# A two-layer decoder trunk: the FFN's block products written out as a software pipeline on VectorE, ScalarE and TensorE

## The chip, the cores and the metric

The kernel runs on one core of a Trainium2 chip. The metric is device time in microseconds (us) of one execution, median of several; lower is better.

## The reference

The computation is a trunk of two layers, each a gated token mixer and then a dense SwiGLU feed-forward network (FFN), on 512 tokens of width 1024, in float32. The change touches the FFN alone:

```python
D_MODEL = 1024; SEQ = 512; DEPTH = 2
FF = ((8 * D_MODEL + 3 * 256 - 1) // (3 * 256)) * 256        # 2816

def _swiglu(h, w_gate_up, w_down):
    gu = jnp.einsum('bsd,df->bsf', h, w_gate_up)
    g, u = gu[..., :FF], gu[..., FF:]
    return jnp.einsum('bsf,fd->bsd', jax.nn.silu(g) * u, w_down)

def reference(x, norm_mix, w_in, w_ret_o, w_sb_o, w_out, norm_ffn, w_gate_up, w_down, norm_final):
    h = x
    for layer in range(DEPTH):
        hn = _rmsnorm(h, norm_mix[layer])
        h = h + _mixer(hn, w_in[layer], w_ret_o[layer], w_sb_o[layer], w_out[layer])
        hn = _rmsnorm(h, norm_ffn[layer])
        h = h + _swiglu(hn, w_gate_up[layer], w_down[layer])
    return _rmsnorm(h, norm_final)
```

## The kernel before

**Numbers.** Every float32 operand of a product is split into a high and a low part. ScalarE (ACT) writes the high part as a rounded copy, VectorE (DVE) subtracts it from the original for the low part, and TensorE (PE) multiplies high x high, low x high and high x low into one PSUM sum. So a weight tile is ready for PE when it has been loaded into a raw buffer (SP issues the load; three buffers, `rawp`), copied by ACT (`whi`, or `w_h` for half a tile) and subtracted by DVE (`wlo`, `w_l`). The wide pairs `whi`, `wlo` have three buffers each.

**The FFN.** The 2816 features are 22 tiles of 128. For each, a gate product and an up product of 512 tokens are made, silu(gate) x up is formed, split (`a_h`, `a_l`), and the down projection sums over features. The first five tiles (PLAIN) are plain: two units of 24 matmuls of 512 columns each. While they run, `pair_input` prepares sums of the normed input for the other seventeen. These, called pairs here (tiles 5 to 21 of a layer), use a product scheme with seven block products in place of eight. A block (`block`, whose matmuls carry L613) is twelve matmuls of 256 columns; a pair is 84. The blocks are named by their weights: A11 and A12 (halves of the gate tile a), A22 (a half of the up tile b), S1 to S4 (sums of halves). Gate and up results, g and u, lie in two PSUM banks: `x` (named g in the trace) takes A11, S2, S3, A22, and `zy` (named a) takes A12, S1, S4. On the way ACT copies two partial sums out of `x`: into `pu` after A11 (L624) and after S2 (L628), each before the next block may add to the same sum; and into `u3` after S3 (L632), which DVE adds to S1's sum (L633). At the end DVE adds `zy` and `pu` (L638), ACT takes silu (L639), DVE multiplies to `a` (L646) and ACT copies `a_h` (L647).

**A pair's weights** (`pair_weights`, L555 to L579) come from two loads, a and b, of 512 KB: `whi`, `wlo` of a (L565, L566; for A11, A12); `s1`, a sum of b's halves (L571); A22's split (L237, L238); two subtractions in place (L573, L574); `whi`, `wlo` of the changed b (S3, S2); S1's split; one more sum (L577); and S4's split. The load of a later tile waits until a raw buffer's last reader is done.

**What sets the order.** A scheduler orders each engine's instructions; the source order is a preference, and the functions are generators that interleave a pair's blocks with the last two of the pair ahead. An engine runs its own list one after the other. `down(0)` (features 0 to 10) comes after pair 12, and `down(1)` after pair 21; each is eight tiles of 33 matmuls of 512 columns, and the first tile of each has its own loop (L700 to L720), since its newest `a_h` comes last.

## Time and profile before

| | |
|---|---|
| median of 3 runs | 1651.94 us (1651.32 to 1652.76) |
| the profiled execution | 1651.83 us, of which its span is 1650.1 us |
| PE busy | 1626.0 us, 99 % of the span |
| DVE, ACT busy | 1134.4 us (69 %), 799.9 us (48 %) |
| granted PE clock, mean | 0.999 of full speed |

The profile is of one execution. PE's busy time uses modelled ends: a matmul of 256 columns is shown as 0.28 us and the next one starts 0.12 us after it, so a small gap doesn't show as idle time. The start times of the timeline do show it. The pairs of the first layer run from 516 to 602 and from 663 to 762 us, those of the second from 1331 to 1417 and from 1478 to 1577 us.

### The profile page before, as it was taken

What the parts mean: (1) busy time and instruction counts of PE and PEld (TensorE: products, weight loads), DVE (VectorE), ACT (ScalarE), POOL (GpSimd) and SP (SyncE); (2) the same over time, 40 slices, a digit from 0 to 9 for tenths busy, and PEclk for the clock granted to TensorE, in tenths of its full rate; (3) what the DMA queues carried; (4) which work ended last, traced back from release to release, by engine and by line L of the source; (5) the groups of instructions that cost most, each with busy time, mean ns of one, the idle gap of its engine ahead of it and who ended that gap; (6) DMA issues with size and microseconds to landing.
All of it is one profiled execution on the core that took longest, in us unless ns stands there. A gap on an engine that the chain in (4) does not pass through costs nothing.

```text
span 1650.1 us, 21859 instructions
## 1 busy us (share of the span) xinstructions
PE 1626.0 (99%) x8665; PEld 1376.0 (83%) x8665; DVE 1134.4 (69%) x1657; ACT 799.9 (48%) x1307; POOL 67.9 (4%) x57
## 2 busy tenths in 40 slices
PE   9999999999999999999999999999999999999998
PEld 7887777888888988998888778888888889889977
DVE  5799878645577774776448987885354877648753
ACT  5667745432354542454327677453234545325543
POOL 2000000000210000000200000000002000000001
PEclk9999999999999999999999999999999999999999
DMA  5322311233222333233332122123222313332332
GB/s 195 103 77 77 101 54 64 90 102 103 92 77 89 97 111 100 86 95 108 111 100 90 64 90 90 63 68 103 99 96 96 103 64 93 111 104 80 97 106 77
DMA packets 47911, 153.62 MB, mean 93 GB/s; under 512 B 5440, under 2 KB 5952, under 8 KB 47808
## 3 DMA queue, kind: packets, MB, share of 16 engines
q1 hardware_dynamic: 45360, 148.00, 27.7%
q10 hardware_dynamic: 2448, 4.22, 0.8%
q8 instruction: 68, 1.11, 0.3%
q14 instruction: 35, 0.29, 0.1%
HBM read 150.10 MB, written 2.10 MB: 92 GB/s over the span
## 4 chain that ended last, share of the span: by engine, by line
PE 86%; DVE 10%; ACT 2%; issue 1%; DMA 0%; ACTq 0%; SPq 0%; DVEq 0%
PE g L84 18%; PE g L83 18%; PE g L85 18%; PE g L613 12%; PE a L613 8%; PE g L115 2%; PE g L116 2%; PE g L117 2%; DVE wlo L69 2%; DVE z L371 1%; PE a L85 1%; DVE rt L299 1%; PE a L84 1%; PE a L83 1%; DVE kl L345 1%
## 5 line engine op out<-in xcount | busy, mean ns | idle before, releaser
L67 ACT ACTIVATE whi<-raw 128x1024 fp32r<-128x1024 f32 (+1 forms) x224 | 220.2, 983 | 445.8 <-PE g L84 270.0
L69 DVE TENSOR_TENSOR wlo<-raw,whi 128x1024 fp32r<-128x1024 f32 (+1 forms) x224 | 255.1, 1141 | 112.4 <-ACT whi L67 111.7
L84 PE MATMUL g<-xl,whi 128*128 128x512 f32 x800 | 312.4, 391 | 0.0
L85 PE MATMUL g<-xh,wlo 128*128 128x512 f32 x800 | 311.8, 390 | 0.0
L83 PE MATMUL g<-xh,whi 128*128 128x512 f32 x800 | 309.9, 391 | 0.7 <-ACT xh L173 0.7
L83 PEld LDWEIGHTS g<-xh,whi 128*128 128x128 f32 x800 | 150.1, 188 | 33.0 <-ACT xh L173 1.6
L85 PEld LDWEIGHTS g<-xh,wlo 128*128 128x128 f32 x800 | 150.2, 188 | 31.0
L84 PEld LDWEIGHTS g<-xl,whi 128*128 128x128 f32 x800 | 150.2, 188 | 30.8
L85 PE MATMUL g<-a_h,wlo 128*128 128x512 f32 (+1 forms) x319 | 122.3, 383 | 1.5 <-DVE wlo L69 1.5
L84 PE MATMUL g<-a_l,whi 128*128 128x512 f32 (+1 forms) x319 | 123.4, 387 | 0.0
L83 PE MATMUL g<-a_h,whi 128*128 128x512 f32 (+1 forms) x319 | 122.7, 385 | 0.0
L232 POOL TENSOR_TENSOR acc<-acc,sq 128x512 f32<-128x512 f32 x34 | 54.1, 1590 | 1074.4 <-ACT sq L231 1073.9
L565 ACT ACTIVATE whi<-raw 128x1024 fp32r<-128x1024 f32 x68 | 69.0, 1055 | 52.0 <-DVE raw L574 46.0
L613 PE MATMUL a<-xf_h,w_l 128*128 128x256 f32 x272 | 79.6, 293 | 3.2 <-DVE w_l L238 2.9
L566 DVE TENSOR_TENSOR wlo<-raw,whi 128x1024 fp32r<-128x1024 f32 x68 | 80.8, 1222 | 1.1 <-ACT whi L565 1.1
L613 PE MATMUL g<-xf_h,whi 128*128 128x256 f32 x272 | 79.8, 293 | 0.3
L613 PE MATMUL g<-xf_h,wlo 128*128 128x256 f32 x272 | 76.3, 281 | 0.0
L613 PE MATMUL g<-xf_l,whi 128*128 128x256 f32 x272 | 76.2, 280 | 0.0
L115 PE MATMUL g<-whi,xh 128*128 128x512 f32 x192 | 74.9, 392 | 1.0 <-ACT v L318 1.0
L117 PE MATMUL g<-wlo,xh 128*128 128x512 f32 x192 | 75.0, 390 | 0.0
L116 PE MATMUL g<-whi,xl 128*128 128x512 f32 x192 | 74.9, 390 | 0.0
L613 PE MATMUL a<-xf_l,w_h 128*128 128x256 f32 x272 | 71.7, 281 | 0.0
(230 smaller groups left out, 3623.5 us busy)
## 6 DMA issues: line engine op xcount, KB each, us to landing
raw<-in_wgu SPq DMA_DIRECT2D x88, 512.0 KB, 3.3
raw<-in_wf SPq DMA_DIRECT2D x76, 512.0 KB, 3.3
raw<-in_wt SPq DMA_DIRECT2D x24, 512.0 KB, 3.3
raw<-in_wdn SPq DMA_DIRECT2D x32, 384.0 KB, 3.2
raw<-in_wdn SPq DMA_DIRECT2D x32, 320.0 KB, 2.9
raw<-in_wro SPq DMA_DIRECT2D x16, 512.0 KB, 3.2
raw<-in_wout SPq DMA_DIRECT2D x16, 512.0 KB, 3.3
raw<-in_wsb SPq DMA_DIRECT2D x8, 512.0 KB, 3.3
```

The costliest lines, as they stand in the source:

```text
L67: self.last_hi = nc.scalar.activation(hi[:, :n], raw[:, :n], AF.Copy).ins
L69: nc.vector.tensor_tensor(out=lo[:, :n], in0=raw[:, :n], in1=hi[:, :n], op=ALU.subtract)
L83: mm(out, lhsT=ah, rhs=bh, start=start, stop=False)
L84: mm(out, lhsT=ah, rhs=bl, start=False, stop=False)
L85: self.last_mm = mm(out, lhsT=al, rhs=bh, start=False, stop=stop).ins
L115: mm(out, lhsT=ah, rhs=bh, start=start, stop=False)
L116: mm(out, lhsT=al, rhs=bh, start=False, stop=False)
L117: mm(out, lhsT=ah, rhs=bl, start=False, stop=stop)
L232: nc.gpsimd.tensor_tensor(out=self.acc, in0=self.acc, in1=sq, op=ALU.add)
L565: nc.scalar.activation(hi, src, AF.Copy)
L566: tt(out=lo, in0=src, in1=hi, op=ALU.subtract)
L613: self.nc.tensor.matmul(out, lhsT=l[:, s], rhs=r, start=start and c == 0 and k == 0, stop=c == 3 and k == 2, skip_group_check=True)
```

## The change

The block products are the same, and so are the matmuls, copies and sums. What is new is their order and who decides it. `act` and `add` issue ACT and DVE work that the scheduler must keep in the source's order, and the first matmul of each block is kept in order too. A call of `step` does pair f on PE: A11, A12, A22 of the pair ahead, S2, S1, S4 of the pair ahead, S3. Between the blocks the generator `pair_weights` makes the weights of pair f+1, in three parts. `turn`, at the head of a step, finishes earlier pairs: `u3` of f-1, the sum with it, and `a`, `a_h` of f-2. For the first pair the weights are made in the last plain tile (PLAIN-1); for pair 12 in `down(0)`'s last tile. `down(0)` now comes after pair 11, whose last two blocks stay open until step 12, and the first tile of `down(1)` takes its own loads (`down_units`) and several `a_l` from the step before. A few slots changed side in SBUF. The diff, cut to its core:

```diff
+    def add(self, out, a, b, op=ALU.add):
+        return self.tc.keep_in_program_order(self.nc.vector.tensor_tensor(out=out, in0=a, in1=b, op=op))
+    def act(self, out, a, f=AF.Copy):
+        return self.tc.keep_in_program_order(self.nc.scalar.activation(out, a, f))
+    def sub(self, out, a, b):
+        return self.add(out, a, b, ALU.subtract)
...
     def pair_weights(self, gate, up):
-        nc, tt = self.nc, self.nc.vector.tensor_tensor
         a, b = self.raw_unit(gate), self.raw_unit(up)
         p, q = slice(0, T), slice(T, 2 * T)
+        wide = lambda: (self.wp.tile([P, 1024], F32R, name="whi", tag="whi"), self.wp.tile([P, 1024], F32R, name="wlo", tag="wlo"))
+        one = lambda n: (self.slot(n + "h", F32R), self.slot(n + "l", F32R))
+        w = {}
+        ah, al = wide()
+        self.act(ah, a)
+        yield w
         s1 = self.slot("s1")
-        def wide(src):
-            hi, lo = self.wp.tile([P, 1024], F32R, name="whi", tag="whi"), self.wp.tile([P, 1024], F32R, name="wlo", tag="wlo")
-            nc.scalar.activation(hi, src, AF.Copy)
-            tt(out=lo, in0=src, in1=hi, op=ALU.subtract)
-            return [(hi[:, s], lo[:, s]) for s in (p, q)]
-        w = {}
-        w["A11"], w["A12"] = wide(a)
-        tt(out=s1, in0=b[:, p], in1=b[:, q], op=ALU.add)
-        w["A22"] = self.split(b[:, q], "w")
-        tt(out=b[:, p], in0=a[:, p], in1=b[:, p], op=ALU.subtract)
-        tt(out=b[:, q], in0=a[:, p], in1=s1, op=ALU.subtract)
-        w["S3"], w["S2"] = wide(b)
-        w["S1"] = self.split(s1, "w")
-        tt(out=a[:, q], in0=a[:, q], in1=b[:, q], op=ALU.add)
-        w["S4"] = self.split(a[:, q], "w")
-        return w
+        self.add(s1, b[:, p], b[:, q])
+        self.sub(al, a, ah)
+        w["A11"], w["A12"] = ((ah[:, s], al[:, s]) for s in (p, q))
+        h, l = w["A22"] = one("a22")
+        self.act(h, b[:, q])
+        h1, l1 = w["S1"] = one("s1")
+        self.act(h1, s1)
+        self.sub(l, b[:, q], h)
+        self.sub(b[:, p], a[:, p], b[:, p])
+        self.sub(b[:, q], a[:, p], s1)
+        bh, bl = wide()
+        self.act(bh, b)
+        self.add(a[:, q], a[:, q], b[:, q])
+        self.sub(l1, s1, h1)
+        self.sub(bl, b, bh)
+        w["S3"], w["S2"] = ((bh[:, s], bl[:, s]) for s in (p, q))
+        yield
+        h, l = w["S4"] = one("s4")
+        self.act(h, a[:, q])
+        self.sub(l, a[:, q], h)
+        yield
...
-                self.nc.tensor.matmul(out, lhsT=l[:, s], rhs=r, start=start and c == 0 and k == 0, stop=c == 3 and k == 2, skip_group_check=True)
-    def pair(self, wgu, f):
-        nc, tt = self.nc, self.nc.vector.tensor_tensor
-        h = T // 2
-        p, q = slice(0, h), slice(h, T)
-        w = self.pair_weights(wgu[2 * f], wgu[2 * f + 1])
-        x, zy = self.bank(), self.abank()
-        t, u3 = self.slot("pu"), self.slot("u3")
-        self.block(x[:, p], w["A11"], "B11", True)
-        nc.scalar.activation(t[:, p], x[:, p], AF.Copy)
-        self.block(zy[:, p], w["A12"], "B21", True)
-        yield
-        self.block(x[:, p], w["S2"], "T2", False)
-        nc.scalar.activation(t[:, q], x[:, p], AF.Copy)
-        self.block(zy[:, q], w["S1"], "T1", True)
-        yield
-        self.block(x[:, p], w["S3"], "T3", False)
-        nc.scalar.activation(u3[:, p], x[:, p], AF.Copy)
-        tt(out=x[:, q], in0=zy[:, q], in1=u3[:, p], op=ALU.add)
-        yield
-        self.block(x[:, p], w["A22"], "T4", False)
-        yield
-        self.block(zy[:, q], w["S4"], "B22", False)
-        tt(out=t, in0=zy, in1=t, op=ALU.add)
-        nc.scalar.activation(t, t, AF.Silu)
-        self.activated(x, t)
-        yield
-    def activated(self, u, g):
-        a, hi = self.slot("a", F32, self.alow()), self.slot("a_h", F32R, self.alow())
-        self.nc.vector.tensor_tensor(out=a, in0=u, in1=g, op=ALU.mult)
-        self.nc.scalar.activation(hi, a, AF.Copy)
+                mm = self.nc.tensor.matmul(out, lhsT=l[:, s], rhs=r, start=start and c == 0 and k == 0, stop=c == 3 and k == 2, skip_group_check=True)
+                if c == 0 and k == 0:
+                    self.tc.keep_in_program_order(mm)
...
+    def turn(self, prep=None):
+        if self.old:
+            x, zy, t, w = self.old
+            u3 = self.slot("u3")
+            self.act(u3[:, : T // 2], x[:, : T // 2])
+        first = next(prep) if prep else None
+        if self.done:
+            self.activated(*self.done, keep=self.tc.keep_in_program_order)
+        if self.old:
+            self.add(x[:, T // 2 :], zy[:, T // 2 :], u3[:, : T // 2])
+        self.open, self.old, self.done = self.old or self.open, None, None
+        return first
+    def last_products(self):
+        x, zy, t, w = self.open
+        self.block(x[:, : T // 2], w["A22"], "T4", False)
+        yield
+        self.block(zy[:, T // 2 :], w["S4"], "B22", False)
+        self.add(t, zy, t)
+        self.act(t, t, AF.Silu)
+        self.done, self.open = (x, t), None
+        yield
+    def step(self, w, prep, other=lambda: None):
+        p, q = slice(0, T // 2), slice(T // 2, T)
+        nxt = self.turn(prep)
+        behind = self.last_products() if self.open else iter(())
+        x, zy, t = self.bank(), self.abank(), self.slot("pu")
+        self.block(x[:, p], w["A11"], "B11", True)
+        self.act(t[:, p], x[:, p])
+        self.block(zy[:, p], w["A12"], "B21", True)
+        if prep:
+            next(prep)
+        else:
+            other()
+        next(behind, None)
+        self.block(x[:, p], w["S2"], "T2", False)
+        self.act(t[:, q], x[:, p])
+        self.block(zy[:, q], w["S1"], "T1", True)
+        if prep:
+            next(prep)
+        next(behind, None)
+        self.block(x[:, p], w["S3"], "T3", False)
+        self.old = x, zy, t, w
+        return nxt
...
+            if f == PLAIN - 1:
+                prep = weights(PLAIN)
+                w = next(prep)
...
+            if f == PLAIN - 1:
+                next(prep), next(prep)
...
-        old = None
-        for f in range(PLAIN, NF):
-            new = self.pair(wgu, f)
-            next(new)
-            if old:
-                next(old)
-            next(new)
-            if old:
-                next(old)
-            next(new)
-            old = new
-            if f == HALF + 1:
-                self.down(wdn, 0, range(KC))
+        for half in range(2):
+            def lows():
+                self.units = self.down_units(wdn, half, 0)
+                for k in range(EARLY):
+                    self.low_part(half * HALF + k)
+            end = (HALF, NF - 1)[half]
+            for f in range(PLAIN if half == 0 else HALF + 1, end):
+                w = self.step(w, weights(f + 1))
+            self.step(w, None, lows)
+            self.turn()
+            if half == 0:
+                w = self.down(wdn, 0, range(KC), lambda: weights(HALF + 1))
         if last:
             self.tc.keep_in_program_order(nc.scalar.preload_act_table_set("sqrt_and_others"))
-        self.down(wdn, 1, range(KC - 1 if last else KC), old, last)
-    def down(self, wdn, half, tiles, old=None, last=False):
+        self.down(wdn, 1, range(KC - 1 if last else KC), None, last)
...
+                behind = self.last_products() if half else iter(())
+                mm, where = nc.tensor.matmul, {f: (u, slice((f - a) * P, (f - a + 1) * P)) for a, b, u in units for f in range(a, b)}
+                def high(f):
+                    u, s = where[f]
+                    for k in range(2):
+                        mm(ps, lhsT=u[k][:, s], rhs=self.ax[f][0], start=f == f0 and k == 0, stop=False)
+                def low(f):
+                    u, s = where[f]
+                    mm(ps, lhsT=u[0][:, s], rhs=self.ax[f][1], start=False, stop=f == f1 - 1)
+                for f in range(f0 + EARLY, f1 - 1):
+                    self.low_part(f)
+                for f in range(f0, f1 - 1):
+                    if f in (f0 + 4, f0 + 6):
+                        next(behind, None)
+                    high(f)
+                if half:
+                    self.activated(*self.done, keep=self.tc.keep_in_program_order)
+                    self.done = None
+                for f in range(f0, f1 - 1):
+                    low(f)
+                self.low_part(f1 - 1)
+                high(f1 - 1)
+                low(f1 - 1)
             else:
+                if weights and i == tiles[-1]:
+                    prep = weights()
+                    w = next(prep)
+                    next(prep), next(prep)
...
```

Three places show what moves. In the rows the names carry tile numbers, `waits` names the queues or engines whose signals an instruction waits for (DMAHW: a load), and a row without `waits` needs none of its own.

DVE, where the first layer's pairs begin, before: from the last plain gate tile (`g_4372`) on. `u_4406` and `a_4408` are tile 4's, `raw_4412` and `raw_4414` are pair 5's a and b, and `wlo_4515` is pair 6's.

```order
L668 TENSOR_TENSOR g_4372<-g_4347,rs_y_3976 128x512 [waits PE_49]
L672 TENSOR_TENSOR u_4406<-g_4381,rs_y_3976 128x512 [waits PE_49]
L571 TENSOR_TENSOR s1_4416<-raw_4414 128x512 [waits DMAHW1_49]
L646 TENSOR_TENSOR a_4408<-u_4406,g_4372 128x512 [waits DVE_49,Activation_49]
L238 TENSOR_TENSOR w_l_4423<-raw_4414,w_h_4422 128x512 [waits Activation_49]
L573 TENSOR_TENSOR raw_4414<-raw_4412,raw_4414 128x512 [waits DVE_49]
L574 TENSOR_TENSOR raw_4414<-raw_4412,s1_4416 128x512 [waits DVE_49]
L238 TENSOR_TENSOR w_l_4433<-s1_4416,w_h_4432 128x512 [waits Activation_49]
L577 TENSOR_TENSOR raw_4412<-raw_4412,raw_4414 128x512 [waits DVE_49]
L566 TENSOR_TENSOR wlo_4429<-raw_4414,whi_4428 128x1024 [waits Activation_49]
L566 TENSOR_TENSOR wlo_4515<-raw_4509,whi_4514 128x1024 [waits DMAHW2_49,Activation_49]
L238 TENSOR_TENSOR w_l_4438<-raw_4412,w_h_4437 128x512 [waits Activation_49]
```

The same place after; `u_4435` and `a_4437` are tile 4's, `raw_4372` and `raw_4374` pair 5's a and b.

```order
L712 TENSOR_TENSOR g_4379<-g_4347,rs_y_3976 128x512 [waits PE_49]
L553 TENSOR_TENSOR s1_4413<-raw_4374 128x512 [waits DMAHW0_49]
L553 TENSOR_TENSOR wlo_4377<-raw_4372,whi_4376 128x1024 [waits DMAHW7_49]
L553 TENSOR_TENSOR a22l_4417<-raw_4374,a22h_4416 128x512 [waits Activation_49]
L553 TENSOR_TENSOR raw_4374<-raw_4372,raw_4374 128x512 [waits DVE_49]
L553 TENSOR_TENSOR raw_4374<-raw_4372,s1_4413 128x512 [waits DVE_49]
L553 TENSOR_TENSOR raw_4372<-raw_4372,raw_4374 128x512 [waits DVE_49]
L553 TENSOR_TENSOR s1l_4420<-s1_4413,s1h_4419 128x512 [waits Activation_49]
L553 TENSOR_TENSOR wlo_4426<-raw_4374,whi_4425 128x1024 [waits Activation_49]
L553 TENSOR_TENSOR s4l_4432<-raw_4372,s4h_4431 128x512 [waits Activation_49]
L718 TENSOR_TENSOR u_4435<-g_4388,rs_y_3976 128x512 [waits PE_49]
L640 TENSOR_TENSOR a_4437<-u_4435,g_4379 128x512 [waits DVE_49]
```

Tile 4's u and a stood ahead of pair 5's weights; now all of pair 5's weights stand ahead of them.

ACT at the same place, before:

```order
L669 ACTIVATE g_4372<-g_4372 128x512 [waits DVE_49]
L237 ACTIVATE w_h_4422<-raw_4414 128x512 [waits DMAHW1_49]
L237 ACTIVATE w_h_4432<-s1_4416 128x512 [waits DVE_49,Activation_49]
L647 ACTIVATE a_h_4409<-a_4408 128x512 [waits DVE_49,PE_49]
L565 ACTIVATE whi_4428<-raw_4414 128x1024 [waits DVE_49,Activation_49]
L565 ACTIVATE whi_4514<-raw_4509 128x1024 [waits DMAHW2_49,PE_49,Activation_49]
L237 ACTIVATE w_h_4437<-raw_4412 128x512 [waits DVE_49]
L624 ACTIVATE pu_4443<-g_4441 128x256 [waits PE_49]
L628 ACTIVATE pu_4443<-g_4441 128x256 [waits PE_49]
L632 ACTIVATE u3_4444<-g_4441 128x256 [waits PE_49]
```

and after; `a_h_4438` is tile 4's, `whi_4445` pair 6's A11 and A12, and the two `pu_4450` are pair 5's copies after A11 and after S2:

```order
L713 ACTIVATE g_4379<-g_4379 128x512 [waits DVE_49]
L556 ACTIVATE s1h_4419<-s1_4413 128x512 [waits DVE_49,Activation_49]
L556 ACTIVATE whi_4425<-raw_4374 128x1024 [waits DVE_49,PE_49,Activation_49]
L556 ACTIVATE s4h_4431<-raw_4372 128x512 [waits DVE_49]
L641 ACTIVATE a_h_4438<-a_4437 128x512 [waits DVE_49,Activation_49]
L556 ACTIVATE whi_4445<-raw_4441 128x1024 [waits DMAHW2_49,PE_49,Activation_49]
L556 ACTIVATE pu_4450<-g_4448 128x256 [waits PE_49]
L556 ACTIVATE a22h_4479<-raw_4443 128x512 [waits DMAHW3_49]
L556 ACTIVATE s1h_4482<-s1_4476 128x512 [waits DVE_49,Activation_49]
L556 ACTIVATE whi_4488<-raw_4443 128x1024 [waits DVE_49,PE_49]
L556 ACTIVATE pu_4450<-g_4448 128x256 [waits PE_49]
```

Pair 5's copies had ahead of them pair 6's first `whi` and S4's `w_h`; now the first has tile 4's `a_h` and pair 6's `whi` ahead of it, and the second also pair 6's A22, S1 and second `whi`.

DVE, a whole step in the middle of the pairs, before (`raw_4509` and `raw_4511` are pair 6's a and b, `wlo_4642` is pair 7's):

```order
L633 TENSOR_TENSOR g_4441<-a_4442,u3_4444 128x256 [waits Activation_49]
L238 TENSOR_TENSOR w_l_4520<-raw_4511,w_h_4519 128x512 [waits Activation_49]
L573 TENSOR_TENSOR raw_4511<-raw_4509,raw_4511 128x512 [waits DVE_49]
L574 TENSOR_TENSOR raw_4511<-raw_4509,s1_4513 128x512 [waits DVE_49]
L238 TENSOR_TENSOR w_l_4530<-s1_4513,w_h_4529 128x512 [waits Activation_49]
L577 TENSOR_TENSOR raw_4509<-raw_4509,raw_4511 128x512 [waits DVE_49]
L566 TENSOR_TENSOR wlo_4526<-raw_4511,whi_4525 128x1024 [waits Activation_49]
L566 TENSOR_TENSOR wlo_4642<-raw_4636,whi_4641 128x1024 [waits DMAHW4_49,PE_49,Activation_49]
L238 TENSOR_TENSOR w_l_4535<-raw_4509,w_h_4534 128x512 [waits Activation_49]
L638 TENSOR_TENSOR pu_4443<-a_4442,pu_4443 128x512 [waits PE_49]
L646 TENSOR_TENSOR a_4618<-g_4441,pu_4443 128x512 [waits Activation_49]
L571 TENSOR_TENSOR s1_4640<-raw_4638 128x512 [waits DMAHW5_49]
```

and after (`raw_4660` and `raw_4662` are pair 8's, `pu_4547` is pair 6's and `g_4545` pair 6's x; pair 7 is on PE):

```order
L553 TENSOR_TENSOR g_4545<-a_4546,u3_4658 128x256 [waits Activation_49]
L553 TENSOR_TENSOR s1_4700<-raw_4662 128x512 [waits DMAHW7_49,DVE_49]
L553 TENSOR_TENSOR wlo_4665<-raw_4660,whi_4664 128x1024 [waits DMAHW6_49,PE_49,Activation_49]
L553 TENSOR_TENSOR a22l_4704<-raw_4662,a22h_4703 128x512 [waits DVE_49,Activation_49]
L553 TENSOR_TENSOR raw_4662<-raw_4660,raw_4662 128x512 [waits DVE_49]
L553 TENSOR_TENSOR raw_4662<-raw_4660,s1_4700 128x512 [waits DVE_49]
L553 TENSOR_TENSOR raw_4660<-raw_4660,raw_4662 128x512 [waits DVE_49]
L553 TENSOR_TENSOR s1l_4707<-s1_4700,s1h_4706 128x512 [waits Activation_49]
L553 TENSOR_TENSOR wlo_4713<-raw_4662,whi_4712 128x1024 [waits Activation_49]
L553 TENSOR_TENSOR s4l_4756<-raw_4660,s4h_4755 128x512 [waits PE_49,Activation_49]
L553 TENSOR_TENSOR pu_4547<-a_4546,pu_4547 128x512 [waits PE_49]
L640 TENSOR_TENSOR a_4794<-g_4545,pu_4547 128x512 [waits Activation_49]
```

Before, a pair's S1, S3 and S2 weights were made while the pair itself was on PE, and only its A11 `wlo` one step ahead; now the whole row belongs to the next pair.

## Rows read from the trace of the kernel before

**Rows 1.** Waits of PE's weight loads, 510 to 770 us: total us, times, longest.
```profile
PEld a L613 <- DVE w_l L238: 4.7, 15, 1.6
PEld g L613 <- ACT pu L628: 3.8, 16, 0.5
```
**Rows 2.** Chain that ended last, 655 to 760 us: start, us, engine, line, instructions.
```profile
663.11 1.43 PE g L613 x12
...
667.36 2.49 PE a L613 x21
...
689.64 2.40 PE g L613 x19
...
742.64 2.39 PE g L613 x19
```
**Rows 3.** Timeline of PE at the first pair: start, us, matmul, idle before it.
```profile
515.79 0.39 PE L85 MATMUL g<-xh,wlo 128*128 128x512 f32 x1
516.02 0.28 PE L613 MATMUL g<-xb_h,whi 128*128 128x256 f32 x1
...
518.87 0.28 PE L613 MATMUL a<-xf_h,w_h 128*128 128x256 f32 x1
520.57 0.38 PE L613 MATMUL a<-xf_h,w_l 128*128 128x256 f32 x1 [1.43 <-DVE w_l L238]
...
523.52 0.39 PE L613 MATMUL g<-xb_h,wlo 128*128 128x256 f32 x1 [0.95 <-DVE wlo L566]
```
**Rows 4.** Timeline of PE in the first tile of down(1), each layer.
```profile
765.35 0.50 PE L713 MATMUL g<-a_h,whi 128*128 128x512 f32 x1 [1.31 <-ACT a_h L647]
...
1580.70 0.50 PE L85 MATMUL g<-a_h,wlo 128*128 128x512 f32 x1 [1.51 <-DVE wlo L69]
```
**Rows 5.** Timeline of DVE in the middle of the pairs, 685 to 712 us.
```profile
697.73 2.36 DVE L566 TENSOR_TENSOR wlo<-raw,whi 128x1024 fp32r<-128x1024 f32 x2
700.00 0.68 DVE L238 TENSOR_TENSOR w_l<-raw,w_h 128x512 fp32r<-128x512 f32 x1
700.61 0.68 DVE L638 TENSOR_TENSOR pu<-a,pu 128x512 f32<-128x512 f32 x1
...
704.78 0.43 DVE L633 TENSOR_TENSOR g<-a,u 128x256 f32<-128x256 f32 x1 [1.44 <-ACT u L632]
```
**Rows 6.** Timeline of ACT there.
```profile
696.63 2.01 ACT L565 ACTIVATE whi<-raw 128x1024 fp32r<-128x1024 f32 x2 [1.44 <-DVE raw L574]
698.54 0.61 ACT L237 ACTIVATE w_h<-raw 128x512 fp32r<-128x512 f32 x1
699.06 0.37 ACT L624 ACTIVATE pu<-g 128x256 f32<-128x256 f32 x1
...
702.21 0.38 ACT L628 ACTIVATE pu<-g 128x256 f32<-128x256 f32 x1 [0.19 <-PE g L613]
```
**Rows 7.** Loads into the raw buffers, issue to landing: 660 to 745, then 518 to 590 us.
```profile
DMA to landing us min/median/max: 3.2/3.7/4.3
DMA to landing us min/median/max: 3.2/4.1/4.8
```
**Rows 8.** Timeline of DVE from the plain tiles into the first pairs.
```profile
512.41 0.69 DVE L238 TENSOR_TENSOR xf_l<-xv,xf_h 128x512 fp32r<-128x512 f32 x1 [0.45 <-ACT xf_h L237]
513.02 0.68 DVE L668 TENSOR_TENSOR g<-g,rs_y 128x512 f32<-128x512 f32 x1
516.22 0.69 DVE L672 TENSOR_TENSOR u<-g,rs_y 128x512 f32<-128x512 f32 x1 [2.51 <-PE g L85]
...
525.71 0.69 DVE L571 TENSOR_TENSOR s<-raw 128x512 f32<-128x512 f32 x1 [1.64 <-DMA raw<-in_wgu]
```
**Rows 9.** Timeline of ACT there.
```profile
518.20 0.63 ACT L647 ACTIVATE a_h<-a 128x512 fp32r<-128x512 f32 x1
...
522.44 0.36 ACT L624 ACTIVATE pu<-g 128x256 f32<-128x256 f32 x1
```
**Rows 10.** Timeline of ACT before down(1) of the second layer.
```profile
1578.05 1.28 ACT L639 ACT_TABLE_LOAD   x1 [2.58 <-DVE pu L638]
```

## What I predicted, and how

> **What bounds the kernel now.** PE does, and in the stretches that the change touches it waits for weights. I read the waits of PE's weight loads around the first layer's pairs first: fifteen waits for a half tile's low part and sixteen for ACT's copy `pu`, near one of each per pair [rows 1]. They look like 8.5 us, but a wait shows only where the weight load stood idle, so I measured from start times. Between 663.11 and 667.36 three blocks run with nothing late: 1.417 us a block, 9.92 for the seven of a pair [rows 2]. Farther on the same place of the chain comes at 689.64 and, five pairs later, at 742.64: 10.60 a pair [rows 2]. So a pair loses 0.68. The PE timeline puts this in three places: S1's low weights, the copy `pu` ahead of S2 or S3, and a little for A11's `wlo`; each stop also costs about 0.1 more, since the matmul after it takes 0.38 or 0.39 where 0.28 is usual [rows 3]. Over both layers there are some 15 such steps each: 30 x 0.68 = **20.4 us**.
>
> Two places lose more. At the first pair PE is idle 1.43 us for S1's low part and 0.95 for pair 6's `wlo` [rows 3]; a matmul is shown 0.16 longer than its pitch (1.417 / 12 = 0.12), so start to start this is 1.59 and 1.11, with 0.4 for slow matmuls behind and beside them: 3.1 a layer, **6.2**. In `down(1)`'s first tile the last pair's `a_h` or a `wlo` is late, 1.31 and 1.51 idle [rows 4]; with 0.16 of shown overlap and 0.11 for the restart that is 1.6 and 1.8: **3.4**. All that can be won is 20.4 + 6.2 + 3.4 = 30.0.
>
> **The change, part by part.** The number of matmuls, copies, sums and loads stays, so nothing is saved as work. PE's order of blocks changes, and blocks cost the same in any order if their weights are there.
>
> *The steady step.* I walked it from the rows. Take t = 0 at A11 of pair f; PE then wants A12 at 1.42, A22 of f-1 at 2.83, S2 at 4.25, S1 at 5.67, S4 of f-1 at 7.08, S3 at 8.50, the next A11 at 9.92. DVE pays 0.605 for a half tile (700.00 to 700.61), 1.135 for a `wlo` (2.27 for two), 0.43 for the 256-column sum [rows 5]. ACT pays 0.955 for a `whi`, 0.52 for a half tile, 0.38 for a copy out of PSUM that starts about 0.2 after the block ends [rows 6].
> - DVE: `a` 0.15 to 0.75, the sum with `u3` to 1.2, `s1` to 1.8, `wlo` of a to 2.9, A22's low to 3.5, the two subtractions to 4.75, the sum and S1's low to 5.95, `wlo` of b to 7.1, S4's low to 7.7; then it waits for S4 of f-1 on PE (8.5) and adds by 9.35. The work is nine half tiles, two `wlo` and one sum: 5.45 + 2.27 + 0.43 = 8.2 of 9.92.
> - ACT: `u3` 0.2 to 0.55, `whi` of a to 1.5, `a_h` to 2.05, `pu` after A11 to 2.45 (PE wants it at 4.25), A22's and S1's high to 3.5, `whi` of b 4.8 to 5.75, `pu` after S2 to 6.25 (wanted at 8.50), S4's high to 6.8, silu 9.4 to 10.05. About 5.7 of 9.92.
> So every weight is there a good part of a step before its block, and the copies have 1.8 and 2.2 us to spare. The three waits of 0.68 go. What is late next is the load of b: SP may issue it when DVE has ended `wlo` of the b before, at 7.1, and the load of the next a follows 0.6 behind, when S4's low is done; `s1` wants b at 1.2 of the next step. With loads of 3.2 (the shortest, [rows 7]) to 3.3 it lands at 0.4 to 0.5, 0.7 early. The loop of that buffer is 6.0 for `s1` to the end of `wlo`, 0.05 for the signal, and the load: 9.35. It binds when the load takes over 3.87.
>
> [...] The rows say that the waits come from the order of DVE and ACT: SP has its buffer in time and PE waits for `w_l`, `pu`, `wlo` [rows 1, 3]. [...]
>
> *The first pair of each layer*, where the trace of before has no such order. DVE began `g` times the norm of tile 4 at 513.02, after a 0.45 wait for ACT that a different order takes away, so about 512.5 [rows 8]. In the new order all of pair 5's weights come next, `s1` to S4's low: with 0.605 and 1.135 each and the `whi` between the subtractions and the last `wlo`, `wlo` of b ends at 519.1, and tile 4's u and `a`, before at 516.22 and just behind [rows 8], follow from 519.6 to 520.9. ACT has `a_h` of tile 4 (at 518.20 before, [rows 9]) ahead of pair 6's `whi` and that ahead of `pu` of pair 5. So `a_h` 520.95, `whi` 521.5, `pu` 522.45 to 522.85. PE starts A11 at 516.02 and has no pair behind, so it wants S2 at 518.85, right behind A12, and S2 adds to the sum that `pu` copies: it starts at 522.9, **4.0 + 0.1 late**. Before, the copy was late too (522.44, [rows 9]), but PE had S1 and pair 6's first blocks to go on with [rows 3]. Then b of pair 6, issued at 519.15, lands at 522.45; `s1` and the work up to the second subtraction take to 526.15, `whi` to 527.25, and only then comes the second `pu`, at 527.5, for an S3 due at 525.7: **1.8 + 0.1**. In step 6 the margin at S3 is 0.5 and grows. So 6.0 a layer, **12.0** in all. From below it costs 3.1 as before; from above, with that load at 4.3 [rows 7], 1.0 more a layer.
>
> *Into and out of `down(0)`.* Pair 11's last blocks stay open and pair 12's weights are made in the last down tile, which has 33 matmuls at a pitch of 0.23 (515.79 to 516.02, [rows 3]), 7.6 us of PE work, and little for DVE. A margin of over 1 us: nothing. If that cover is gone, a stall like that of the first pair, at most 3.1 a layer.
>
> *The first tile of `down(1)`.* PE does the high products of ten features (20 x 0.23) with two blocks (2.83) between, then ten low ones: 9.7 before the last feature is needed. The last pair's S4 ends at 5.6; sum, silu, `a` and `a_h` follow until 8.5 and `a_l` until 9.2. So layer 1 loses nothing. In layer 2 a table load of 1.28 [rows 10] and a `whi` stand between: `a_h` 10.2, `a_l` 11.1, a loss of **1.2**. Bounds: 0 and the 3.4 of before.
>
> Sum: 30.0 - 12.0 - 1.2 = 16.8 gained. Against the profiled execution, 1651.83 (span 1650.1 and 1.7 around it; 0.1 under the median): **1635.0**.
>
> **The rivals.**
> 1. *The start is as cheap as before.* If `pu` isn't held up (say the load or the `a` of tile 4 comes earlier), the starts cost 6.2: 30.0 - 6.2 - 1.2 = 22.6, **1629.2**. For it: ACT and DVE have slack before 516 [rows 8]. Against: the order of the rows is fixed, and the `a` of tile 4 is behind nine operations.
> 2. *One wait stays in every step.* One of about 0.28 (0.17 and the restart), or a load of 4.2 (step 10.25): 30 x 0.28 = 8.4 given back, **1643.4**. For it: an engine that keeps its order can't fill a wait, and the load's median is 3.7 to 4.1 over both kinds [rows 7].
> 3. *The load of b sets the step, and the kernel is slower.* The load of a is now issued 0.6 behind that of b, both 512 KB, so they share the way for longer. If b takes 4.8, the longest of [rows 7], the step is 6.05 + 4.8 = 10.85, 0.25 over before's: 30 x 0.25 = 7.5, and 5.8 more at the starts, less 2.2 at the end: +11.1, **1663**. It breaks even at a step of 10.48, a load of 4.43. Against: these loads come in pairs before too, half of them land within 3.7 [rows 7], and the load of b is the first of its pair.
> 4. *It does next to nothing*, since a load of about 4.4 takes back nearly all that the waits gave (rival 3's break-even): about **1650**.
>
> **How the numbers follow.** Forecast 0.58, rival 1 0.13, rival 2 0.14, rival 3 0.09, rival 4 0.06. Forecast, 1 and 2 make 0.85, so the range runs from 1627 to 1645: the first two rivals with 2 us for the bounds of the starts. Faster by over 0.2 % (3.3 us, about what a measurement of this kernel can tell from no change) are forecast and rivals 1 and 2: 0.85; the same 0.06; slower 0.09.
>
> **What would show it.** In the changed profile the chain should have a stride of 9.9 in the middle of the pairs, and PE's waits for low parts, `pu` and `wlo` be gone there. At S2 of the first pair PE should be idle about 4 us with ACT's `pu` named, and about 1.8 at its S3. A stride of 10.2 or more with DVE's `s1` waiting for a load is rival 3's mechanism; a stride of 10.2 with another name is rival 2. No wait at S2 of the first pair is rival 1. The forecast is wrong above all if the start costs far from 6 us a layer.

## The result

The changed kernel takes 1634.59 us (median of four runs, 1633.70 to 1634.72) where the kernel before, run beside it, took 1651.76 (four runs). The ratio is 0.9894, with a 95% interval of 0.9877 to 0.9911. The forecast was 1635.0, range 1627 to 1645. One execution of e10 below was slow (2272.95 us, at a granted clock of 0.65) and is left out of its figure.

| | before | after |
|---|---|---|
| the profiled execution | 1651.83 us, span 1650.1 | 1633.70 us, span 1632.0 |
| PE busy | 1626.0 us, 99 % | 1608.4 us, 99 % |
| DVE, ACT busy | 1134.4 us, 799.9 us | 1134.3 us, 793.2 us |

PE, DVE and ACT run as many instructions as before (8665, 1657 and 1307). PE's busy time fell because, as shown in the profile, it takes in the small gaps between matmuls, and there are fewer of them. The waits of PE's weight loads in the new kernel, 510 to 770 us, are one row (engine, output, line, awaited; total us, times, longest); [rows 1] had fifteen waits for `w_l` and sixteen for `pu` in that stretch:

```profile
PEld g L632 <- ACT pu L556: 4.7, 2, 4.5
```

In the chain that ended last (start, us, engine, output and line, instructions), A12 of a pair begins at

```profile
661.14 1.42 PE a L632 x12
671.03 1.42 PE a L632 x12
680.91 1.42 PE a L632 x12
...
740.24 1.42 PE a L632 x12
```

Eight steps take 79.10 us, 9.89 each, where [rows 2] gave 10.60. That is 0.71 less, and over some 30 steps 21.3 us.

The first pair, in PE's timeline (start, us, matmul, idle before it):

```profile
515.91 0.28 PE L632 MATMUL g<-xb_h,whi 128*128 128x256 f32 x1
...
518.65 0.28 PE L632 MATMUL a<-xf_l,whi 128*128 128x256 f32 x1
523.19 0.39 PE L632 MATMUL g<-xf_h,whi 128*128 128x256 f32 x1 [4.26 <-ACT pu L556]
...
524.04 0.41 PE L632 MATMUL g<-xf_l,whi 128*128 128x256 f32 x1
524.25 0.41 PE L632 MATMUL g<-xf_h,whi 128*128 128x256 f32 x1
...
527.53 0.28 PE L632 MATMUL a<-xf_l,s1h 128*128 128x256 f32 x1
527.83 0.39 PE L632 MATMUL g<-xf_h,whi 128*128 128x256 f32 x1
```

S2 waits 4.26 us for ACT's `pu`, as forecast, where [rows 3] had 1.43 and 0.95 for other things. What follows was not forecast. From 523.8 the matmuls start 0.21 apart instead of 0.12, and only at 527.2 are they back. The stretches of the profile show why (from and to, us, busy time of PE, PE's loads, DVE, ACT and POOL, then the granted clock of PE as a share, the DMA share and GB/s):

```profile
515.90:518.80 2.90, 2.90 (x25) 2.81 (x23) 2.87 (x5) 1.58 (x2) 0.00 (x0) 1.00 0.00 0
518.80:523.10 4.30, 0.13 (x2) 0.00 (x0) 2.74 (x5) 1.81 (x4) 0.00 (x0) 1.00 0.65 229
523.20:527.00 3.80, 3.80 (x19) 3.80 (x20) 3.77 (x7) 1.53 (x3) 0.00 (x0) 0.56 0.03 10
527.20:532.00 4.80, 4.78 (x41) 4.58 (x40) 2.65 (x4) 2.81 (x6) 0.00 (x0) 1.00 0.45 141
```

After a pause of 4.3 us the granted clock is 0.56 of full speed in the next 3.8 us. It fell only after PE had begun again: the row of the pause itself still has 1.00, S2's first four matmuls start at 523.19, 523.41, 523.53 and 523.65, at the old pitch but for the restart, and the stretch from 523.80 to 527.20 alone has 0.52. S2 and S1 take 4.46 us, from 523.19 to 527.65, instead of 2.83. S3's wait, which I had put at 1.8, is then only 0.2.

On ACT the order of the wait is to be read off (start, us, ...):

```profile
521.29 0.63 ACT L641 ACTIVATE a_h<-a 128x512 fp32r<-128x512 f32 x1 [2.79 <-DVE a L640]
521.82 1.04 ACT L556 ACTIVATE whi<-raw 128x1024 fp32r<-128x1024 f32 x1
522.77 0.36 ACT L556 ACTIVATE pu<-g 128x256 f32<-128x256 f32 x1
...
526.44 1.06 ACT L556 ACTIVATE whi<-raw 128x1024 fp32r<-128x1024 f32 x1 [2.27 <-DVE raw L553]
527.40 0.37 ACT L556 ACTIVATE pu<-g 128x256 f32<-128x256 f32 x1
```

`pu` was ready to run at 517.5 and ran at 522.77, behind `a_h` of tile 4 and pair 6's `whi`. The second one ran at 527.40, behind pair 6's second `whi`.

In the middle of the pairs DVE now waits for a load in every step:

```profile
681.56 0.69 DVE L553 TENSOR_TENSOR s<-raw 128x512 f32<-128x512 f32 x1 [0.58 <-DMA raw<-in_wgu]
...
686.44 1.22 DVE L553 TENSOR_TENSOR wlo<-raw,whi 128x1024 fp32r<-128x1024 f32 x1
...
691.35 0.69 DVE L553 TENSOR_TENSOR s<-raw 128x512 f32<-128x512 f32 x1 [0.70 <-DMA raw<-in_wgu]
```

From `s1` to the end of the second `wlo` (687.66) is 6.1 us, and the next b is there 3.7 later. The sum, 9.8, is just under PE's 9.89, and nothing on PE waits for it.

At the end, in the second layer, `down(1)`'s first tile waited 1.51 in [rows 4]. Now PE's timeline there reads

```profile
1562.11 2.48 PE L762 MATMUL g<-a_l,whi 128*128 128x512 f32 x10
1564.43 0.40 PE L84 MATMUL g<-a_h,whi 128*128 128x512 f32 x1
1564.67 0.40 PE L85 MATMUL g<-a_l,whi 128*128 128x512 f32 x1
1565.02 0.50 PE L758 MATMUL g<-a_h,whi 128*128 128x512 f32 x1
```

The ten low products end, then come two products of the next tile (L84, L85), and only then the last feature's (L758), 0.13 late and with 0.11 for the restart. In the first layer nothing is late.

### The profile page after: what moved, and what is told of

Same layout as the page of the kernel before. It is cut to its first block, busy times and chain, and to the rows that moved or that the text cites. A ratio compares the mean times of both kernels' runs of the same rounds, so it can differ in the third digit from the quotient of the medians.

```text
span 1632.0 us, 21885 instructions
## 1 busy us (share of the span) xinstructions
PE 1608.4 (99%) x8665; PEld 1374.0 (84%) x8665; DVE 1134.3 (70%) x1657; ACT 793.2 (49%) x1307; POOL 67.9 (4%) x57
## 4 chain that ended last, share of the span: by engine, by line
PE 87%; DVE 10%; ACT 2%; issue 1%; DMA 0%; SPq 0%; DVEq 0%; ACTq 0%
PE g L85 18%; PE g L84 18%; PE g L86 18%; PE g L632 12%; PE a L632 9%; PE g L116 2%; PE g L117 2%; PE g L118 2%; DVE wlo L70 2%; PE g L758 1%; DVE z L372 1%; PE a L86 1%; DVE rt L300 1%; PE a L85 1%; PE a L84 1%
## 5 line engine op out<-in xcount | busy, mean ns | idle before, releaser
L85 PE MATMUL g<-xl,whi 128*128 128x512 f32 x800 | 312.5, 391 | 0.1
L84 PE MATMUL g<-xh,whi 128*128 128x512 f32 x800 | 310.0, 391 | 0.2 <-ACT whi L197 0.2
L84 PEld LDWEIGHTS g<-xh,whi 128*128 128x128 f32 x800 | 150.1, 188 | 32.5 <-ACT xh L174 0.9
L85 PEld LDWEIGHTS g<-xl,whi 128*128 128x128 f32 x800 | 150.2, 188 | 31.2 <-DVE xl L176 0.5
L85 PE MATMUL g<-a_l,whi 128*128 128x512 f32 (+1 forms) x319 | 123.2, 386 | 0.0
L84 PE MATMUL g<-a_h,whi 128*128 128x512 f32 (+1 forms) x319 | 123.1, 386 | 0.0
L84 PEld LDWEIGHTS g<-a_h,whi 128*128 128x128 f32 x319 | 59.9, 188 | 12.7
L86 PEld LDWEIGHTS g<-a_h,wlo 128*128 128x128 f32 x319 | 59.9, 188 | 12.5
```

The costliest lines, as they stand in the source:

```text
L84: mm(out, lhsT=ah, rhs=bh, start=start, stop=False)
L85: mm(out, lhsT=ah, rhs=bl, start=False, stop=False)
L86: self.last_mm = mm(out, lhsT=al, rhs=bh, start=False, stop=stop).ins
```

## The experiments

All ten are compared by their medians (e4 has one execution only), and by one length: from the start of the first block of a layer's pairs to the first product of `down(0)`. The 47 blocks between take 66.4 us at 9.89 / 7 each, so what is over is the price of the start. In e4 only 42 blocks stand there, so its figures are over 59.3, and they hold its longer steps too. The kernel before, run beside each group, took 1651.92 (e1 to e4), 1652.35 (e5 to e8) and 1652.47 us (e9, e10): between groups, differences under 1 us say nothing.

| kernel | time, us | over 66.4 (e4: 59.3), layer 1 | layer 2 |
|---|---|---|---|
| before | 1651.9 | | |
| after | 1634.59 | 6.4 | 6.5 |
| e1, scheduler decides | 1628.89 | 3.2 | 3.5 |
| e2, before with four raw buffers | 1650.73 | | |
| e3, after with four raw buffers | 1634.15 | 6.9 | 6.0 |
| e4, longer load of b | 1714.28 | 24.5 | 20.8 |
| e5, first copy ahead | 1640.31 | 9.8 | 9.2 |
| e6, second copy ahead | 1634.76 | 6.9 | 6.9 |
| e7, start rewritten | 1624.06 | 1.2 | 1.2 |
| e8, e7 with three raw buffers | 1636.07 | 8.1 | 6.3 |
| e9, e7 with tile 4 later | 1622.50 | 0.4 | 0.4 |
| e10, e1 with four raw buffers and tile 4's up weights first | 1624.60 | 1.2 | 1.2 |

My theory: the repeating wait went because a pair's weights are made a step ahead; the start is what the change costs, and its length comes from ACT's order and the load of pair 6's b. Rivals: the wait came from too few raw buffers; or it is the kept order that took it away.

**e1: the weights a step ahead, the order free.**

```diff
-        return self.tc.keep_in_program_order(self.nc.vector.tensor_tensor(out=out, in0=a, in1=b, op=op))
+        return (self.nc.vector.tensor_tensor(out=out, in0=a, in1=b, op=op))
...
-        return self.tc.keep_in_program_order(self.nc.scalar.activation(out, a, f))
+        return self.nc.scalar.activation(out, a, f)
...
-                    self.tc.keep_in_program_order(mm)
+                    pass
```

(and the same for `a` and `a_h`.) 

> The changed kernel, but nothing is kept in the source's order: the scheduler places VectorE, ScalarE and the blocks, and the weights are still written one step ahead. My theory: the 0.68 us of each step went because a pair's weights are made in the step ahead of it, so most steps stay near 9.9 us, and the scheduler puts S1 and pair 6's first blocks into the stall at the first pair, which then costs 3 to 4 us a layer instead of 6.6: 1627 to 1634. Rival, that the kept order is what took the waits away: steps of 10.3 to 10.6 and 1643 to 1652.

It took 1628.89, 5.7 us less than the changed kernel. In its chain A12 of three pairs begins at

```profile
547.38 1.42 PE a L632 x12
...
557.31 1.42 PE a L632 x12
...
567.20 1.42 PE a L632 x12
```

so its step is 9.9 too. Its waits in PE's weight loads, 510 to 770 us:

```profile
PEld g L632 <- DVE wlo L553: 1.8, 1, 1.8
PEld g L632 <- ACT pu L556: 0.7, 3, 0.2
```

The rival falls: writing the weights a step ahead takes the repeating wait away, and keeping the order adds 3 us to each start. The scheduler put S1 and the beginning of pair 6 behind A12, where the kept order makes PE wait for S2. e1 still has the other moves of the source (the place of `u3`, `a` and `a_h`); no run takes these out by themselves.

**e2: the kernel before with four raw buffers.**

```diff
-        self.rawp = pool("rawp", 3)
+        self.rawp = pool("rawp", 4)
...
-        self.slots = pool("slots", 39)
+        self.slots = pool("slots", 37)
```

> The kernel before with four raw buffers instead of three, and two fewer of the 39 half-tile slots to make room. My theory: the repeating wait of the kernel before comes from the order of VectorE and ScalarE, so the step stays 10.6 and the time within 3 us of 1651.8. Rival, too few buffers: the steps fall to about 9.9 and the time to about 1631.

1650.73 against 1651.92, ratio 0.9992 with an interval of 0.9983 to 1.0001. The step in its chain, and its waits:

```profile
711.29 2.41 PE g L613 x19
721.89 2.41 PE g L613 x19
```

```profile
PEld a L613 <- DVE w_l L238: 4.7, 15, 1.6
PEld g L613 <- ACT pu L628: 3.4, 16, 0.2
```

10.60 a step and the same sixteen and fifteen waits as [rows 1, 2]: the raw buffers are not what these gaps wait for. The other pools were not tried with more, but they are of the same size in the changed kernel, which has no such gap.

**e3: the changed kernel with four raw buffers** (the same two lines). 

> The changed kernel with four raw buffers instead of three and two fewer slots. My theory: VectorE's wait of 0.6 to 0.7 us a step for the load of b goes, but PE's step stays 9.89, since PE waits for nothing there. At the first pair the load of pair 6's b now takes the buffer of pair 5's a, which is free when S4's low part is done, 0.6 us later than before, so S3 of the first pair is 0.6 later in each layer: 1635 to 1637. Rival, that the load sets something on the path: faster than 1632.

1634.15, the same as the changed kernel. As expected the time and the step (9.89) stay, and DVE's wait for b goes. At the start I was wrong about the load: with the fourth buffer pair 6's b was issued at 508.72 and landed at 511.94, early instead of 0.6 late. So `s1` of pair 6 begins with no wait, and DVE waits for ACT's first `whi` of pair 6 instead, which stands behind tile 4's `a_h`:

```profile
521.95 0.69 DVE L553 TENSOR_TENSOR s<-raw 128x512 f32<-128x512 f32 x1
523.67 1.23 DVE L553 TENSOR_TENSOR wlo<-raw,whi 128x1024 fp32r<-128x1024 f32 x1 [1.04 <-ACT whi L556]
```

The second `pu` runs at 527.76, 11.0 after the first block of the pairs, where it was 11.5. PE gains nothing by it in layer 1. The chain at the first pair shows the two blocks after the pause, S2 and S1, and then S3:

```profile
523.96 2.93 PE g L632 x12
526.89 2.56 PE a L632 x12
529.45 2.84 PE g L632 x24
```

By their start times S2 and S1 take 5.3 us (523.96 to 529.25) for two blocks of 1.42; the execution's mean granted clock is 0.995. S3 follows without a wait: the slow stretch alone puts it 12.5 after the first block, 0.6 later than the second `pu` put it in the changed kernel. In layer 2 the two blocks take 4.5 us and S3 has no wait either. That is why layer 1's start is 0.5 longer and layer 2's 0.5 shorter, where I expected 0.6 longer in both.

**e4: a longer load of b.**

```diff
-        a, b = self.raw_unit(gate), self.raw_unit(up)
+        a, b = self.raw_unit(gate), self.rawp.tile([P, 1024], F32, name="raw", tag="raw")
+        self.nc.sync.dma_start(out=b[:, :64], in_=up[:, :64])
+        self.nc.sync.dma_start(out=b, in_=up)
```

> The changed kernel with a longer load of each pair's b: 64 columns of it are loaded first and then all of it into the same buffer, so that the whole takes some 5.5 to 6.5 us instead of 3.6. The result is the same. My theory: the loop of load, s1 to the end of the second wlo (6.1 us) and back to the load sets the step from a load of 3.8 on, so the step is 6.1 plus the load, 11.6 to 12.6, and the time 1690 to 1720. Rival, that the loads are hidden: step 9.9 and 1635.

1714.28, of one execution. DVE's `s1` in two steps:

```profile
699.13 0.69 DVE L553 TENSOR_TENSOR s<-raw 128x512 f32<-128x512 f32 x1 [3.09 <-DMA raw<-in_wgu]
...
711.31 0.69 DVE L553 TENSOR_TENSOR s<-raw 128x512 f32<-128x512 f32 x1 [3.06 <-DMA raw<-in_wgu]
```

12.18 a step, which is 6.1 and a load of 6.1. So the loop of rival 3 is real. The kernel took 80 us more, and 30 steps of 2.29 more make 69 of them. By the same sum the loop meets PE's 9.89 at a load of 3.8, an estimate that no run tried closely. The changed kernel, with 3.7, stands just on the other side.

**e5: the first copy ahead.** In the first step ACT copies `pu` before pair 6's `whi` and tile 4's `a_h`:

```diff
-        nxt = self.turn(prep)
+        first = not self.old and not self.open
+        if not first:
+            nxt = self.turn(prep)
...
         self.act(t[:, p], x[:, p])
+        if first:
+            nxt = self.turn(prep)
...
+            if f == PLAIN - 1:
+                self.done = (us, gs)
+                continue
             self.activated(us, gs)
```

> The changed kernel with one thing moved in the first pair of each layer: the copy pu after A11 stands ahead of pair 6's first whi and of tile 4's a_h on ScalarE. My theory: S2 then waits only some 0.5 us, for pair 5's second wlo at 519.3, but S3 still wants the second copy, which stands behind pair 6's second whi and so behind its load of b, at 527.4. So PE idles 5.5 us at S3 instead of 4.4 at S2, and the slow stretch of TensorE's clock that follows such a pause falls on blocks that nothing hides: 1.5 to 2 us more in each layer, 1636 to 1639. Rival, that the pause at S2 is a cost by itself: 1626 to 1628.

1640.31, 5.7 us slower than the changed kernel and 1.3 over what I expected. S3 is where it waits, and the blocks after it run at a granted clock of 0.50:

```profile
529.27 0.58 PE L632 MATMUL g<-xf_h,whi 128*128 128x256 f32 x1 [6.76 <-ACT pu L556]
...
529.30:533.00 3.70, 3.70 (x17) 3.70 (x18) 1.91 (x3) 1.20 (x3) 0.00 (x0) 0.50 0.43 134
```

(The last line is the row of that stretch.) S2's pause of 4.3 had cost nothing by itself: S3 had to wait for the second copy anyway, and this single longer pause left a slow stretch that no other wait hid. Pair 6's b also landed later here: its `s1` started at 524.16, in the changed kernel at 522.72, though the load was issued at nearly the same time. Why is open. Against the changed kernel the starts are 3.4 and 2.7 us longer: S3 begins 1.2 and 0.4 later after the first block, and the two blocks after the pause take 2.4 and 2.5 more than the usual 2.83. I had put that stretch at 1.5 to 2.

**e6: the second copy ahead.** The generator yields once more before the second `whi`, and the first step issues it after the copy:

```diff
         self.sub(b[:, q], a[:, p], s1)
+        yield
         bh, bl = wide()
...
         self.act(t[:, q], x[:, p])
+        if prep and first:
+            next(prep)
```

> The changed kernel with the other copy of the first pair moved: pu after S2 stands ahead of pair 6's second whi on ScalarE; the pause of 4.4 us at S2 stays. My theory: after the pause S2 and S1 run at the slow clock and end at 527.5 anyway, so S3 starts at most 0.3 us earlier: 1634 to 1635. Rival, that the second copy costs the 1.9 us a layer of my prediction: 1631.

1634.76: nothing. In layer 1 the second copy runs as soon as S2 has ended, S2 and S1 take 5.3 us again (523.32 to 528.60), and S3 begins with no wait:

```profile
526.28 0.38 ACT L556 ACTIVATE pu<-g 128x256 f32<-128x256 f32 x1 [1.84 <-PE g L633]
...
528.60 0.32 PE L633 MATMUL g<-xf_h,whi 128*128 128x256 f32 x1
```

In layer 2 the two blocks take 4.5, and what that gives is lost at pair 6's S3, where PE is idle 0.22 for `pu`. So neither copy alone can be blamed for the 6.4 us. Each covers the other, and the slow stretch covers the second.

**e7: the start rewritten.** Four raw buffers, tile 4's up weights made before pair 5's (so that pair 6's loads find free buffers early; e3 shows that the fourth buffer alone does that for b), the first copy ahead in the first step, the second copy ahead in every step, and tile 4's u and `a` behind pair 6's first weights:

```diff
+            src = wgu[2 * f + 1]
             if f == PLAIN - 1:
+                src = self.unit(src)
                 prep = weights(PLAIN)
...
         self.act(t[:, q], x[:, p])
+        late, self.late = self.late, None
+        if late:
+            u, rb, gs = late
+            us, a, hi = self.slot("u"), self.slot("a"), self.slot("a_h", F32R)
+            self.add(us, u, rb, ALU.mult)
+            self.add(a, us, gs, ALU.mult)
+        if prep and first:
+            next(prep)
+        if late:
+            self.act(hi, a)
+            self.ax.append((hi, a))
```

> The changed kernel with a start written anew: four raw buffers and two fewer slots; tile 4's up weights made before pair 5's; both copies pu of a pair ahead of the next pair's whi that held them up (the second one in every step); tile 4's u, a and a_h moved behind pair 6's first weights. My theory: at the first pair PE waits 0.5 us for pair 5's second wlo and for nothing else, so about 6 us a layer go: 1622 to 1625. Rival, that the weights of the first pairs come too late whatever the copies do, so that a later step of each layer waits instead: 1630 to 1634.

1624.06, as expected. The one wait left at the start is another than I had named:

```profile
527.52 0.39 PE L633 MATMUL g<-xf_h,a22h 128*128 128x256 f32 x1 [0.97 <-DVE g L553]
```

A22 of the first pair adds to x after DVE's sum with `u3`, and DVE was behind with pair 6's weights and tile 4. PE has no longer pause at this start, and no slow stretch: from 527.75 on the matmuls start 0.12 apart again, and the execution's mean granted clock is 0.999, where the changed kernel's is 0.996.

**e8: the same with three raw buffers.**

```diff
-        self.rawp = pool("rawp", 4)
+        self.rawp = pool("rawp", 3)
```

> The kernel of the run before with three raw buffers (and the two fewer slots). Now the second whi waits in every step for the copy pu after S2, so s1 to the end of the second wlo takes some 7.2 us instead of 6.1. My theory: the loop of load and weights, 3.6 + 7.2 = 10.8, sets the step, 0.9 over 9.89, less at the first pair: 1645 to 1655. Rival, that the buffers don't matter since PE's weights are a step ahead: 1622 to 1626.

1636.07, neither the one nor the other. The fourth buffer is worth 12 us, but all of it at the start (with three, pair 6's b landed at 524.12 in layer 1, with four at 505.81): in the middle the step is 9.89, not 10.8. My sum had a phase wrong. I had let `s1` begin 1.2 us into the step; it begins 2.1 in (681.56 in the changed kernel, whose step began at 679.5), because it waits for the load. So the second `whi` is due when S2 has just ended, and the copy ahead of it costs next to nothing:

```profile
697.48 0.39 ACT L556 ACTIVATE pu<-g 128x256 f32<-128x256 f32 x1 [2.05 <-PE g L633]
697.76 1.05 ACT L556 ACTIVATE whi<-raw 128x1024 fp32r<-128x1024 f32 x1
```

(DVE's second subtraction, which this `whi` needs as well, ended at 697.64.)

**e9: tile 4 later.** e7 with tile 4's u, `a` and `a_h` one step later, so that DVE reaches the sum with `u3` earlier:

```diff
-        late, self.late = self.late, None
+        late = self.late if not fresh else None
         if late:
+            self.late = None
```

(`fresh` is true in the first step.) 

> The kernel with the rewritten start (e7) with one thing moved: tile 4's u, a and a_h one step later, behind pair 7's subtractions, so that VectorE reaches the sum with u3 of the first pair earlier. In e7 PE waited 1.1 us for that sum at A22 of the first pair. My theory: this wait goes in both layers, 2.2 us: 1621.5 to 1622.5. Rival, that VectorE is behind by as much anyway and the wait only moves: 1624.

1622.50, at the slow edge of the forecast; the wait for the sum falls to

```profile
PEld g L633 <- DVE g L553: 0.3, 1, 0.3
```

This is the fastest version run: 0.9818 of the kernel before (0.9804 to 0.9833) and 12.1 us under the changed kernel. Its interval overlaps e7's (0.9814 to 0.9844); that it is faster rests on the trace, where each start is 0.8 us shorter.

**e10: free order, four raw buffers, tile 4's up weights first** (e1 with e3's two lines and the first hunk of e7). 

> The kernel of e1, in which nothing is kept in the source's order, with four raw buffers, two fewer slots and tile 4's up weights made before pair 5's, as in e7. My theory: what the kept order costs is the start, and what the start needs is the early load of pair 6; with both, PE waits less than the 2.5 us a layer of e1, and the steps stay at 9.89: 1624 to 1628. Rival, that without the kept order the buffers change nothing: 1629.

1624.60, 4.3 us less than e1, and the start is as short as e7's. So the fourth buffer and the early weights of tile 4 together are worth that much under a free order too, and without the kept order the time is within 0.6 us of e7's.

## Why the prediction was right, and where its steps were not

The time was 0.4 us from the forecast, and the two large terms hold. By the two spans, 18.1 us went; the medians say 17.2. That it came so close is in part luck: the steps gave 0.9 more than forecast and `down(1)` 1.0 more, and the starts cost 0.9 more.

- **The steady step: right.** Forecast 9.92, measured 9.89; 21.3 us for 20.4. That it isn't the kept order or the raw buffers is shown by e1 (without the kept order the step is the same) and e2 (with four raw buffers and the old order it isn't). What is left is the source that makes the weights a step ahead, with the small moves named at e1. The rival of one wait a step is dead.
- **The load of b: the step that was mis-sized.** I put it at 3.2 to 3.3 us and b 0.7 early. It took 3.5 to 3.8 there, and DVE waits 0.6 to 0.7 for b, which comes 3.7 after the last `wlo`. Why it takes longer is open. Rival 3's reason, the load of a issued 0.6 behind it, isn't enough: in e3 and e7 two loads are issued as close, and the median load is 3.3. So the loop is 9.8 and not 9.35, and the margin to PE's step 0.1 and not 0.55. It did no harm, since the loop still ends before PE's step does and the weights are some 6 us ahead (the second `wlo` ends at 687.66; the pair's S2 comes 4.25 after its A11 at 689.4). e4 shows the price where it binds. Rival 3's loop is there, and the kernel stands nearer its edge than the chance of 0.09 said.
- **The first pair: right in size, wrong in its parts.** Forecast 6.0 a layer, measured 6.4. The forecast had a wait of 4.0 at S2 and 1.8 at S3. Measured were 4.42 (523.19 less 518.65, less one pitch), then 1.6 of slow clock and restart on S2 and S1 (4.46 for 2.83), then 0.3 at S3, its restart included. That the slow stretch costs here about what the wait it hides would have cost is chance: e3 and e6 take that wait away and keep the time. The step that failed is the one that priced a pause by its length alone. A pause of 1.43 in [rows 3] left no slow stretch (granted clock 1.00 from 520.50 to 524.30); that row was no guide to one of 4.
- **Rival 1** (a start as cheap as before) didn't happen in this kernel, but e1 shows that it was there to be had: 3.2 to 3.5 a layer.
- **`down(0)`: nothing**, as forecast; no wait of PE stands there.
- **`down(1)`'s first tile: mis-sized.** 1.2 forecast in layer 2, 0.24 measured. I had held PE to the source's order. These products are not kept in order, and the scheduler had put two of the next tile ahead of the last feature, which filled most of the wait: `a_h` ended at 1564.97, 10.3 us after the tile's first product, much as the 10.2 forecast. In layer 1, nothing, as forecast.

Put together: 21.3 from the steps, 3.2 from the ends (3.4 less 0.24), less 6.7 for the starts (twice 6.45 less 3.1), makes 17.8, for 18.1 measured by the spans. What the ends gave is read from the trace alone; no run takes that part of the change out.

## What to carry to other kernels

When a pipeline is written out, its steady step is the easy half: walk the first step by itself, with an engine's whole queue, since there each engine has another's work behind it and nothing to go on with. A wait that can be read off may cover a second one of the same length, so try moving both before blaming either. And write down the slack of each loop that a buffer closes; one that runs at 9.8 under a bound of 9.89 looks free until a load grows: at 6.1 us, in e4, the step was 12.18.

## What the runs showed of the hardware

- After pauses of 4.3 and 6.8 us PE's granted clock was 0.56 and 0.50 over the next 3.8 and 3.7 us. Two blocks that take 2.83 us took 4.5 to 5.3. In the first layer of the changed kernel the clock fell 0.5 us after PE had begun again (0.79 from 523.50 to 523.80, 0.52 from there to 527.20); in e5's it had fallen during the pause (0.88 from 522.50 to 529.20). After the pause of 1.43 us in [rows 3] the clock stayed at 1.00 (520.50 to 524.30), and after that of 0.97 us in e7 the matmuls kept starting 0.12 apart. So these pauses of 4.3 us and more cost their length and 1.6 to 2.5 us besides, unless another wait covered it. Between 1.43 and 4.3 us the length alone doesn't tell. In e4's one execution a pause of 1.89 us was followed by a clock of 0.55 over the next 3.8 us, and one of 2.78 us by 1.00; why is open:

```profile
778.65 0.45 PE L634 MATMUL g<-xf_h,whi 128*128 128x256 f32 x1 [1.89 <-ACT pu L556]
...
1623.72 0.39 PE L634 MATMUL g<-xf_h,whi 128*128 128x256 f32 x1 [2.78 <-ACT pu L556]
```

```profile
778.65:782.45 3.80, 3.80 (x19) 3.80 (x20) 2.17 (x4) 1.38 (x3) 0.00 (x0) 0.55 0.45 144
1623.72:1627.52 3.80, 3.80 (x32) 3.80 (x33) 3.29 (x5) 2.10 (x4) 0.00 (x0) 1.00 0.45 149
```

- In the changed kernel the load of a pair's b, with the next a issued 0.6 us behind, mostly landed in 3.4 to 3.8 us, and the median of all 512 KB loads of this weight is 3.6, where it was 3.3 before. How close the loads are issued is not the cause by itself: with four raw buffers they are as close, and the median is 3.3 again (e3, e7, e9); with three it is 3.6 and 3.7 (after and e8). Why is open. The issue rows, after and in e3:

```profile
raw<-in_wgu SPq DMA_DIRECT2D x88, 512.0 KB, 3.6
raw<-in_wgu SPq DMA_DIRECT2D x88, 512.0 KB, 3.3
```
